# Four more weight tiles, six units ahead or in use, and units given back one by one, in a two-layer decoder trunk on one core

## The chip, the cores and the metric

The kernel runs on one core of one Trainium2 chip. The metric is the time of one execution on the device, in microseconds. The engines are called TensorE (PE, and PEld for its weight loads), VectorE (DVE), ScalarE (ACT), GpSimd (POOL) and SyncE (SP), as in the profile.

## The reference

Two layers work on 512 tokens of width 1024. In each layer, `x` is normalised and multiplied by one wide input matrix, whose columns feed three mixers and their gates; the mixers' outputs are gated, projected, added up, multiplied by `w_out` and added to `x`:

```
h    = rmsnorm(x, norm_g)
proj = h @ w_in        # columns: rq rk rv rz | sq sk sv sz | cu cz | ga gb gc
y_a  = retention(rq, rk, rv)       * silu(rz)
y_b  = stick_breaking(sq, sk, sv)  * silu(sz)
y_c  = s5_ssm(cu)                  * silu(cz)   # with its own product, w_glu
merged = sigmoid(ga)*(y_a @ proj_a) + sigmoid(gb)*(y_b @ proj_b) + sigmoid(gc)*(y_c @ proj_c)
x    = x + merged @ w_out
```

Retention works in chunks of 128 tokens with 4 heads. Stick-breaking attention has 8 heads, four pairs here; it needs, for each query, a running product over the keys of sigmoid(-z), and multiplies it by sigmoid(z). The state-space mixer keeps 64 complex states for each of 32 groups of channels. All is float32.

## The kernel before, in words

**Weights.** All weights of both layers come as 196 units of 128 x 1024 numbers (98 a layer), in the order in which they are used. A unit is loaded by SP's queue into a tile `raw`. ScalarE rounds it into `wh` (line 318), VectorE subtracts that from `raw` and leaves the rest in `wl` (helper line 197): this pair is a unit that is made. Each product is then three matmuls, high by high, high by low, low by high (`three`). `raw`, `wh` and `wl` share one pool of W_TILES = 12 tiles of 4 KB per partition; a tile is free again when its last reader in the program has run. Up to RAW_BUFS = 4 tiles are `raw`, and up to W_BUFS = 4 units may be made and not yet given back: 4 x 2 + 4 = 12.

The class `Weights` counts: `made`, `free` (units given back), `loaded`. `room(n)` asks whether n more tiles fit, `fill()` makes units as long as `made < free + W_BUFS` and there is room, and loads after each, `take()` hands out the next unit and makes it if it isn't there.

**Pieces.** The program is written out by hand as a list of pieces, each of 24 matmuls of 512 columns (12 for the products with 4 blocks), and the order of instructions on every engine is the order in which they are written; the engines wait for each other by semaphores alone. ORDER_TEXT sets the order. A product *by tokens* (sk, sq, sv, cu, rq, rk, rv0, rv1, out0, out1) has four pieces, one for each 128 tokens, and each piece reads all four of its units: `token_major` takes four units ahead of its first piece and gives them back, all four, at the end of its fourth. A product *by channels* (sz, gb, cz, gc, ga, rz, pa, and glu, pb, pc with two pieces to a unit) takes one unit, which is given back after the piece (`channel_piece`, counted at the end of the main loop's turn).

Numbered from 0, a layer has the pieces sk 0 to 3, sq 4 to 7, sv 8 to 11, sz:1 12, ..., gb:6 23, cu 24 to 27, cz:0 28, ..., rq 48 to 51, rk 52 to 55, rv0 56 to 59, rv1 60 to 63, glu from 64, ..., out0 100 to 103, out1 104 to 107; the second layer's sk begins with 108.

**What is written around a piece.** In the main loop's turn for a piece, first come the steps that are due in it: the generators of the mixers and evacuations, each of which says after how many pieces it goes on. A step that says 0 has issued small matmuls and goes on "late", in the same turn behind the piece: it evacuates what they gave. Then comes the piece itself, `m()`, then the late steps, then `W.fill()`, then "background" work (the state-space coefficients), until the estimated load of VectorE or GpSimd for this turn is reached.

So, for one piece, ScalarE and VectorE see: due steps, late steps, conversions of weights, background.

**The steps that the text speaks of.**
- Stick-breaking, `sb_pair`: for each head, scores `z` (TensorE), `kp` and `w` = sigmoid of both signs (ScalarE, lines 1047 and 1048), a scan along `kp` and a product into `w` (VectorE, line 1051 and the helper), in a late step; later the transposes `wt` of these `w` (TensorE, line 1068, `turn`) as a due step ahead of a piece. Pair 3 has its second head's scores in piece 27 and the transposes of it ahead of piece 28.
- State-space: `U` (line 867) evacuates cu; `win` (line 729) is a matrix turned by TensorE; `ut` (line 883) is `U` turned, and `S<-ut,win` uses both a piece later; `mt` (line 801) are copies on GpSimd of `kk`, which VectorE makes.
- Normalising, `normalise`: a token block of `x` is turned by TensorE (line 398), and ScalarE and VectorE evacuate it as `hh` (line 421) and `hl`, the operands of all products of the layer. At the start this is written out with the first four conversions between (`first_x`); in the last pieces of out1 it makes the next layer's.

Of the kernel before, what the change touches and what calls it, by code (L numbers as in the profile page):

```python
# [21 lines left out]
NT = 4  # L22
# [12 lines left out]

K = dict(

    nw=12, w=4, raw=4, b=48,

    sb0=0, sb_gap=4, ssm0=6, ssm_gap=3, ret0=9, ret_gap=3, x0=-3, x1=2, ret_pre=4, lead=9,  # L40

# [145 lines left out]
def trunk(ctx: ExitStack, tc, x_in, w_in, par_in, bc_in, ng_in, cst_in, rope_in, out):  # L187
    nc = tc.nc
# [33 lines left out]
    def pmm():  # L222
        return ps_mm.tile([P, 512], F32, tag="mm", name="mm")
# [47 lines left out]
    def then(gen):  # L271

        spawn(gen, now[0] + 1, True)
# [61 lines left out]
    W = Weights()  # L335
    between = []

    def three(ps, a, b, first, last):

        MM(ps, a[0], b[0], start=first, stop=False)  # L340
        MM(ps, a[0], b[1], start=False, stop=False)
        MM(ps, a[1], b[0], start=False, stop=last)
# [10 lines left out]
    def token_major(lhs, evac):  # L353

        units = []

        def piece(t):
            if not units:
                units.extend(W.take() for _ in range(4))
            ps = pmm()  # L360
            for k in range(8):
                if k == 4 and between:
                    between.pop()()
                w = units[k // 2]
                sl = slice(512 * (k % 2), 512 * (k % 2) + 512)
                three(ps, lhs(k, t), (w[0][:, sl], w[1][:, sl]), k == 0, k == 7)
            if t == NT - 1:
                W.free += 4
            then(evac(t, ps))

        return [lambda t=t: piece(t) for t in range(NT)]
# [1020 lines left out]
```

## Time and profile before

| | |
|---|---|
| three runs | 1311.26 us median (1310.98 to 1312.12) |
| the profiled execution | 1311.17 us, span 1309.5 us |
| TensorE busy | 1271.7 us (97%), granted clock 0.992 over the span |
| VectorE, ScalarE, GpSimd busy | 855.6 us (65%), 537.6 us (41%), 382.5 us (29%) |
| DMA queues | two of kind hardware_dynamic (29,664 and 7,632 packets), two of kind instruction (50 and 29) |

A row of a timeline gives the start in microseconds from the span's start, the duration, engine, line, operation, the tile written and those read, their shapes, a count of instructions merged, and in brackets the idle time of the engine just before and what ended it. For a matmul the streamed operand stands first: `mm<-wh,hh` is a product by tokens, `mm<-hh,wh` one by channels. A row of a stretch gives its length and then busy time and number of instructions of PE, PEld, DVE, ACT and POOL, the granted clock of TensorE as a share of 2.4 GHz, the busy share of the DMA engines and GB/s.

### The profile page before, as it was taken

How to read it: one execution, taken by the hardware profiler on the slowest of the kernel's cores; microseconds unless marked ns; L12 is line 12 of the kernel's file. 1: busy time of each engine (PE TensorE's matmuls, PEld its weight loads, DVE VectorE, ACT ScalarE, POOL GpSimd, SP SyncE). 2: the span in 40 equal slices, each digit the busy share in tenths (PEclk: the TensorE clock that was granted, in tenths of full speed). 3: DMA queues.
4: the chain of work that ended last, by engine and by line, in shares of the span. 5: the costliest groups of instructions: out<-in, count | busy, mean ns of one | idle time of the engine just before them, and what ended most of it. 6: DMA issues, size and time to landing. Idle time of an engine off the chain costs nothing. (4 is left out here: it accounts for less than half of the span.)

```text
span 1309.5 us, 16640 instructions
## 1 busy us (share of the span) xinstructions
PE 1271.7 (97%) x6360; PEld 1048.5 (80%) x6360; DVE 855.6 (65%) x1189; ACT 537.6 (41%) x919; POOL 382.5 (29%) x452
## 2 busy tenths in 40 slices
PE   6989989999999999999999999899999999999998
PEld 5867768788887888888888877788888878888887
DVE  5997678776785438556365576789657844575542
ACT  5445534445343534332244445344534534423311
POOL 3340036638442012000042000584555311210000
PEclk9989989999999999999999999899999999999999
DMA  6232221222322322234433222122241232222342
GB/s 223 90 124 77 65 65 49 81 81 89 119 68 65 104 77 77 81 97 141 161 118 127 81 65 71 43 81 65 84 127 65 65 120 90 65 74 88 97 135 75
DMA packets 37375, 120.05 MB, mean 92 GB/s; under 512 B 4144, under 2 KB 4528, under 8 KB 37296
## 3 DMA queue, kind: packets, MB, share of 16 engines
q1 hardware_dynamic: 29664, 105.40, 25.2%
q10 hardware_dynamic: 7632, 13.59, 3.1%
q8 instruction: 50, 0.82, 0.3%
q14 instruction: 29, 0.24, 0.1%
HBM read 114.78 MB, written 4.19 MB: 91 GB/s over the span
## 5 line engine op out<-in xcount | busy, mean ns | idle before, releaser
L197 DVE TENSOR_TENSOR wl<-raw,wh 128x1024 fp32r<-128x1024 f32 x196 | 251.6, 1294 | 114.6 <-ACT wh L318 111.8
L197 PE MATMUL mm<-hh,wh 128*128 128x512 f32 x640 | 256.0, 400 | 0.0
L197 PE MATMUL mm<-hh,wl 128*128 128x512 f32 x640 | 251.2, 393 | 4.9 <-DVE wl L197 4.9
L197 PE MATMUL mm<-hl,wh 128*128 128x512 f32 x640 | 250.7, 392 | 0.0
L318 ACT ACTIVATE wh<-raw 128x1024 fp32r<-128x1024 f32 x196 | 205.8, 1057 | 86.7 <-PE mm L197 38.9
L197 PE MATMUL mm<-wh,hh 128*128 128x512 f32 x512 | 207.5, 405 | 0.9 <-ACT hh L421 0.9
L197 PE MATMUL mm<-wl,hh 128*128 128x512 f32 x512 | 202.6, 396 | 4.3 <-DVE wl L197 4.3
L197 PE MATMUL mm<-wh,hl 128*128 128x512 f32 x512 | 202.0, 395 | 0.0
L197 PEld LDWEIGHTS mm<-hh,wl 128*128 128x128 f32 x640 | 120.8, 189 | 32.2 <-DVE wl L197 6.3
L197 PEld LDWEIGHTS mm<-hh,wh 128*128 128x128 f32 x640 | 121.0, 189 | 25.1 <-issue 1.6
L197 PEld LDWEIGHTS mm<-hl,wh 128*128 128x128 f32 x640 | 121.0, 189 | 23.5
L197 PEld LDWEIGHTS mm<-wl,hh 128*128 128x128 f32 x512 | 104.5, 204 | 24.5 <-DVE wl L197 7.8
L197 PEld LDWEIGHTS mm<-wh,hh 128*128 128x128 f32 x512 | 104.5, 204 | 19.0 <-ACT hh L421 1.3
L197 PEld LDWEIGHTS mm<-wh,hl 128*128 128x128 f32 x512 | 104.2, 204 | 18.4 <-DVE hl L197 0.3
L1051 DVE TENSOR_TENSOR_SCAN kp<-kp,zero 128x511 f32<-128x511 f32 (+1 forms) x64 | 67.6, 1076 | 26.2 <-ACT kp L1047 26.1
L994 ACT ACTIVATE gate<-mm 128x512 f32<-128x512 f32 x48 | 28.6, 596 | 114.2 <-PE mm L197 114.2
L197 POOL TENSOR_SCALAR ms<-ss 128x8 f32<-128x8 f32 (+3 forms) x56 | 19.1, 341 | 181.5 <-DVE ss L824 100.6
L197 POOL TENSOR_TENSOR rs<-ms,mhalf 128x8 f32<-128x8 f32 (+3 forms) x56 | 64.6, 1154 | 4.7
L1033 POOL CAST qd<-qd 64x512 fp32r<-64x512 f32 x16 | 16.3, 1016 | 134.1 <-ACT qd L1028 133.7
L822 ACT ACTIVATE sq<-mm 128x512 f32<-128x512 f32 x32 | 19.0, 593 | 84.6 <-PE mm L197 84.5
L197 PE MATMUL mm<-wl,mgh 128*128 128x512 f32 x128 | 50.1, 391 | 0.2
L197 PE MATMUL mm<-wh,mgh 128*128 128x512 f32 x128 | 49.9, 390 | 0.0
(253 smaller groups left out, 2263.2 us busy)
## 6 DMA issues: line engine op xcount, KB each, us to landing
raw<-in_w SPq DMA_DIRECT2D x196, 512.0 KB, 3.5
x<-in_x SPq DMA_DIRECT2D x8, 256.0 KB, 7.3
rope<-in_rope ACTq DMA_DIRECT2D x8, 256.0 KB, 3.7
xh<-in_x ACTq DMA_DIRECT2D x8, 256.0 KB, 4.4
x<-xh ACTq DMA_DIRECT2D x8, 256.0 KB, 2.0
xh<-x ACTq DMA_DIRECT2D x8, 256.0 KB, 4.6
out<-xh ACTq DMA_DIRECT2D x8, 256.0 KB, 2.1
gB<-in_ng SPq DMA_DIRECT2D x2, 256.0 KB, 5.8
```

What stands on the lines that cost most here:

```text
L197: return f(*a, **k)
L318: ACT(wh, raw, AF.Copy)
L822: ACT(s2, ps, AF.Square)
L994: ACT(sg, ps, AF.Sigmoid)
L1033: nc.gpsimd.tensor_copy(out=qd[h][o, :], in_=qd[h][r, :])
L1051: nc.vector.tensor_tensor_scan(v, v, zero1.to_broadcast([P, n - 1]), 1.0, ALU.mult, ALU.add)
```

## The change

The pool has 16 tiles instead of 12, and up to six units may be made and not given back. The room comes from a part of SBUF that is set aside for descriptors written by GpSimd, which the kernel doesn't use: 512 bytes per partition of it are left. And a product by tokens gives a unit back, and calls `fill()`, in its fourth piece after every second of the eight blocks, instead of giving back all four behind it.

```
--- before.py
+++ after.py
@@ -35,7 +35,7 @@
 
 K = dict(
 
-    nw=12, w=4, raw=4, b=48,
+    nw=16, w=6, raw=4, b=48,
 
     sb0=0, sb_gap=4, ssm0=6, ssm_gap=3, ret0=9, ret_gap=3, x0=-3, x1=2, ret_pre=4, lead=9,
 
@@ -364,8 +364,10 @@
                 w = units[k // 2]
                 sl = slice(512 * (k % 2), 512 * (k % 2) + 512)
                 three(ps, lhs(k, t), (w[0][:, sl], w[1][:, sl]), k == 0, k == 7)
-            if t == NT - 1:
-                W.free += 4
+                if t == NT - 1 and k % 2:
+
+                    W.free += 1
+                    W.fill()
             then(evac(t, ps))
 
         return [lambda t=t: piece(t) for t in range(NT)]
@@ -1378,7 +1380,7 @@
     from concourse.bass_utils import run_bass_kernel_spmd as _run
 
     ins = _layout({k: np.asarray(v) for k, v in inputs.items()})
-    nc = _bacc.Bacc("TRN2", target_bir_lowering=False, num_devices=1)
+    nc = _bacc.Bacc("TRN2", target_bir_lowering=False, num_devices=1, dynamic_dma_scratch_size=512)
     arrays, args = {}, []
     for name in _INS:
         a = np.ascontiguousarray(ins[name])
```

## Rows read from the trace of the kernel before

**Rows 1.** TensorE's waits: engine, line, waited for; us in total, times, longest.

```profile
PE wt L1068 <- DVE w L197: 13.5, 8, 3.1
...
PE mm L197 <- DVE wl L197: 9.2, 7, 3.3
```

**Rows 2.** Stretches of time; busy time by engine, granted clock, DMA share, GB/s.

```profile
80.00:100.00 20.00, 15.91 (x60) 12.16 (x59) 17.98 (x18) 9.77 (x13) 12.93 (x13) 0.83 0.35 117
...
90.89:104.72 13.83, 12.26 (x47) 9.90 (x48) 11.03 (x13) 8.15 (x12) 2.46 (x3) 0.76 0.13 39
...
189.00:198.00 9.00, 9.00 (x39) 8.19 (x37) 4.22 (x5) 1.49 (x6) 0.72 (x1) 0.77 0.19 60
...
220.00:240.00 20.00, 19.06 (x93) 14.70 (x93) 15.78 (x17) 9.47 (x20) 16.86 (x19) 1.00 0.40 132
...
400.00:420.00 20.00, 17.88 (x83) 14.23 (x82) 12.71 (x10) 9.24 (x14) 7.29 (x4) 1.00 0.33 106
```

**Rows 3.** TensorE's timeline, sv to sz and pair 0: start, duration, tile<-operands, [idle].

```profile
92.46 0.79 PE L197 MATMUL mm<-hh,wl 128*128 128x512 f32 x1 [3.30 <-DVE wl L197]
...
107.12 1.04 PE L1068 MATMUL wt<-ident,w 128*128 128x128 f32 x8
```

**Rows 4.** The page's groups, the subtraction: busy, mean ns | idle before, releaser.

```profile
L197 DVE TENSOR_TENSOR wl<-raw,wh 128x1024 fp32r<-128x1024 f32 x196 | 251.6, 1294 | 114.6 <-ACT wh L318 111.8
```

**Rows 5.** VectorE's timeline in the first stage.

```profile
30.84 0.69 DVE L824 TENSOR_REDUCE ss<-sq 128x8 f32<-128x512 f32 x1 [0.81 <-ACT sq L822]
...
90.89 5.53 DVE L197 TENSOR_TENSOR wl<-raw,wh 128x1024 fp32r<-128x1024 f32 x4
...
104.29 0.43 DVE L197 TENSOR_TENSOR w<-w,kp 128x255 f32<-128x255 f32 x1
```

**Rows 6.** ScalarE's timeline in piece 27, the last of cu.

```profile
214.89 1.12 ACT L729 ACTIVATE win<-T 128x512 f32<-128x512 f32 x2
...
218.28 1.06 ACT L318 ACTIVATE wh<-raw 128x1024 fp32r<-128x1024 f32 x1 [0.73 <-PE mm L197]
...
227.70 0.76 ACT L867 ACTIVATE U<-mm 128x128 f32<-128x128 f32 x4
```

**Rows 7.** TensorE's timeline: after two stick-breaking waits, pieces 27 and 28, and S.

```profile
188.40 2.18 PE L1068 MATMUL wt<-ident,w 128*128 128x128 f32 x9 [2.41 <-DVE w L197]
...
197.06 0.40 PE L197 MATMUL mm<-wh,hl 128*128 128x512 f32 x1
...
222.31 0.40 PE L197 MATMUL mm<-wh,hl 128*128 128x512 f32 x1
...
222.55 1.62 PE L1068 MATMUL wt<-ident,w 128*128 128x128 f32 x10
...
230.32 0.39 PE L197 MATMUL mm<-hh,wl 128*128 128x512 f32 x1
...
356.44 2.00 PE L197 MATMUL S<-ut,win 128*128 128x64 f32 x16
```

**Rows 8.** VectorE's timeline: first scan and last product of two heads.

```profile
118.50 1.27 DVE L1051 TENSOR_TENSOR_SCAN kp<-kp,zero 128x127 f32<-128x127 f32 x2
...
121.27 0.42 DVE L197 TENSOR_TENSOR w<-w,kp 128x255 f32<-128x255 f32 x1
...
216.54 2.73 DVE L1051 TENSOR_TENSOR_SCAN kp<-kp,zero 128x127 f32<-128x127 f32 x2 [1.08 <-ACT kp L1047]
...
222.48 0.42 DVE L197 TENSOR_TENSOR w<-w,kp 128x255 f32<-128x255 f32 x1
```

**Rows 9.** GpSimd's timeline behind piece 27.

```profile
224.30 6.47 POOL L801 COPY mt<-kk 32x256 f32<-32x256 f32 x8 [2.47 <-DVE kk L197]
```

**Rows 10.** Late steps of pieces 51 and 107, and what stands ahead of piece 108.

```profile
349.22 1.55 ACT L883 ACTIVATE ut<-T 64x256 f32<-64x256 f32 x4
...
659.94 1.06 ACT L421 ACTIVATE hh<-T 128x512 fp32r<-128x512 f32 x2
...
664.38 1.03 PE L398 MATMUL T<-ident,xn 128*128 128x128 f32 x8
```

More of the change, by code (lines that the diff above doesn't have):

```diff
@@ L36 @@
 K = dict(
-    nw=12, w=4, raw=4, b=48,
+    nw=16, w=6, raw=4, b=48,
     sb0=0, sb_gap=4, ssm0=6, ssm_gap=3, ret0=9, ret_gap=3, x0=-3, x1=2, ret_pre=4, lead=9,
@@ L366, in piece @@
                 three(ps, lhs(k, t), (w[0][:, sl], w[1][:, sl]), k == 0, k == 7)
-            if t == NT - 1:
-                W.free += 4
+                if t == NT - 1 and k % 2:
+                    W.free += 1
+                    W.fill()
             then(evac(t, ps))
@@ L1380 @@
     ins = _layout({k: np.asarray(v) for k, v in inputs.items()})
-    nc = _bacc.Bacc("TRN2", target_bir_lowering=False, num_devices=1)
+    nc = _bacc.Bacc("TRN2", target_bir_lowering=False, num_devices=1, dynamic_dma_scratch_size=512)
     arrays, args = {}, []
```

## The prediction

> **What bounds the kernel now.** I read the shares of busy time first: TensorE is busy nearly throughout, so the time is its stream of products plus the places where it stands. Then TensorE's list of waits [rows 1]: two causes carry most of it, `wt` (transposes of stick-breaking weights) waiting for VectorE's `w`, and products waiting for the low part `wl` of a weight unit. Only the second is a matter of weights being late. The list has no places, so next came stretches of time [rows 2]: 80 to 100 has 15.91 us of products and a clock of 0.83; 220 to 240 loses 0.94 us, 400 to 420 loses 2.12, and the second layer repeats these two once each. TensorE's timeline names the pieces: sv to sz:1 at 92.46 [rows 3], cu to cz:0 near 225, rv0 to rv1 near 410. Each is an end of a product by tokens, which holds all four units that may exist until its last piece. Last came what ScalarE and VectorE do in those last pieces, because the change puts instructions there.
>
> **The change part by part.** *Six units instead of four.* The conversions per piece are worked out from the program's counters: a piece that makes one unit still makes one, the last piece of each product by tokens still makes four, but piece 0 makes two more, and from there each unit is made two units earlier. So the first two units of the next product are ready before its turn.
>
> (a) sv to sz:1. The 3.30 us wait at 92.46 goes [rows 3]; what is late next is VectorE itself. The two subtractions added in piece 0 cost it 2 x 1.29 = 2.6 us [rows 4], and it has hardly a gap from 30.84 on; the idle 0.81 us before 30.84 takes some of that up, so at piece 11 it is about 1.8 us late: the four subtractions that begin at 90.89 begin at 92.7 [rows 5]. From there to the last `w` that pair 0 needs (104.29 + 0.43) VectorE works 11.03 of 13.83 us [rows 2]; the rest was waiting for results of TensorE, which now comes earlier. So that `w` is there at 92.7 + 11.0 = 103.7, and the `wt` of 107.12 [rows 3] can run 3.4 us sooner. Gain 3.4 us. Bounds: nothing (VectorE as far behind as TensorE), and 5.7 us (the 3.30 us and some 2.4 us of products at the low clock behind it: 0.76 over the 13.83 us).
>
> (b) rv0 to rv1: the 2.12 us of 400 to 420 [rows 2] go, in both layers, since units one and two are ready and three and four are wanted only half a piece later. Gain 4.2 us; bounds 2 and 4.2.
>
> (c) Piece 0 itself. The two added conversions stand on ScalarE and VectorE ahead of the normalising of token blocks 2 and 3. I take nothing, as block 2 is wanted only by piece 2; bounds 0 and the 1.8 us by which VectorE then runs late.
>
> *Giving back one by one.* Before, the four conversions of a last piece came after that piece's "late" steps (evacuations of small products that are issued ahead of the piece). Now they are issued inside the piece, so ahead of the late steps, on ScalarE and VectorE alike. And with 6 x 2 + 4 = 16 tiles all taken, a conversion can only write into the two tiles of the unit just given back: it waits until TensorE has read that unit. The fourth therefore starts when the piece ends, and everything late is queued behind it. That ScalarE's queue holds later work back shows in rows 6: `U` could be evacuated after the last product of the piece at 222.31 [rows 7], and ran at 227.70, behind the conversions. What stands there in each last piece:
>
> (d) cu, piece 27 (and its twin in layer 2): the late steps are two copies `win`, the sigmoids `kp` and `w` of pair 3's second head, and VectorE's scans and products on them, and TensorE's next instructions are the transposes `wt` of just these. Today `win` starts at 214.89 [rows 6], the scans and products run from 216.54 to 222.90 [rows 8], and `wt` follows at 222.55 without a wait [rows 7]: no cover is left. After: the last read of the fourth unit is the product at 222.31; its conversion runs from 222.5 to 223.56 (1.06 long, as the one at 218.28 [rows 6]); the scan starts as far behind `win` as now, 216.54 - 214.89 = 1.65, so at 225.2. The chain of scans and products takes 118.50 to 121.69 = 3.19 us in pair 0 and 6.36 us here [rows 8]. GpSimd, busy beside it today, is idle for 2.47 us before 224.30, and what it does then waits for steps behind this chain [rows 9]; so I take 3.19: `w` at 228.4. One transpose runs a little before; nine are left. The nearest row for nine transposes and 24 products after such a wait is 188.40 to 197.06 + 0.24 = 8.9 us [rows 7], in which the granted clock was 0.77 [rows 2], that is, part of it at 1.2 GHz. So piece 28 ends at 228.4 + 8.9 = 237.3, against 230.32 + 0.23 = 230.55, with today's 0.94 us for `wl` already in the latter. Loss 6.7 us, twice: 13.4. Bounds per place: 4.4 (no time at the low clock: less 0.9 for the transposes and 1.4 for the products) and 9.9 (chain of 6.36).
>
> The two lengths of the chain are 3.2 us apart, and a rule says which to take. The Trainium skill, "SBUF — State Buffer", section "Who interferes with whom": a VectorE instruction with two SBUF inputs shuts out, and is shut out by, a GpSimd instruction that reads SBUF. By the row at the same place the time would be 1326.6, by the rule, with GpSimd idle, it stays as summed below.
>
> (e) rq, piece 51, twice: the late step is the copies `ut`, 1.55 us [rows 10], wanted by `S` at 356.44 [rows 7]. The piece's last read is at 354.4, the conversion ends at 355.5, `ut` at 357.1. Loss 0.7 us each, 1.4; bounds 0 and 1.5.
>
> (f) out1, piece 107, once: the late step is `hh` and then `hl` of the next layer's first token block [rows 10]. After the piece's end come 0.2 + 1.06 us for the conversion, 1.29 for its subtraction on VectorE and 0.6 for the first `hl`, 3.2 us; TensorE wants it some 1.4 us after the end (eight transposes of block 1, 1.03 [rows 10], and two products). Loss 1.8 us; bounds 0 and 2.3.
>
> sk, sv, rv1 and out0 have no late steps in the last piece. sq, rk and rv0 have copies that nobody wants within a piece: nothing, hidden by pieces of 5.5 us; 0.5 each if the PSUM banks they hold ran out. The first piece of a product no longer makes a unit ahead of its late steps; nothing on the path waits for those there.
>
> *The scratch.* The page lists no queue whose descriptors GpSimd writes: nothing. The loads in SP's queue keep their order; at the start four more find fresh tiles, so no load waits longer than now.
>
> **Sum.** -3.4 - 4.2 + 13.4 + 1.4 + 1.8 = +9.0 us. The profiled execution took 1311.17 us (span 1309.5, 1.7 around it), 0.1 under the median of the runs, so 1320.2, say 1320.
>
> **The rivals.**
> 1. *Not slower: the late steps of piece 27 aren't held.* If its conversions wrote to tiles that are free early, they would run behind the piece's first `U`, from 215.0, and be done at 219.2; `w` would come at 219.2 + 1.65 + 3.19 = 224.0, 1.5 us after `wt` wants it, less the 0.94 saved: +0.6 at each place, and nothing for (e) and (f). -3.4 - 4.2 + 1.2: 1304.8. It decides by the end of the fourth conversion: before some 222.4 the gains win. For it: the wait of `wh` for TensorE is short today. Against: the count of sixteen. Chance 0.11.
> 2. *The clock doesn't fall behind the new waits, and the first stage gives back its whole 5.7 us.* 2 x 4.4 + 1.4 + 1.8 - 5.7 - 4.2 = +2.1: 1313.3. For it: VectorE is idle for 2.8 of the 13.83 us. Against: the stand in (d) is longer than the 3.30 us at 92.46, behind which the clock is down. Chance 0.15.
> 3. *GpSimd's work moves along with the chain*, which is 6.36 long again: 2 x 3.2 more, 1326.6. Against: rows 9. Chance 0.13.
> 4. *VectorE is the bound of the first stage,* and its 2.6 us push TensorE as far as the ready units pull: (a) is nothing, 1323.6. For it: 17.98 of 20 us in 80 to 100. Chance 0.13.
>
> My forecast has 0.48.
>
> **How the numbers follow.** The forecast, 3 and 4 are slower by over 0.2% (2.6 us, about what a measurement of this kernel tells from no change): 0.74. Of 2, two thirds lie within 0.2% and a third above. Slower 0.79, same 0.10, faster 0.11. The low end of the range is (d) at 4.4 with (a) at 5.7 and (e), (f) at nothing, 1310; the high end is rival 3, 1327. Rival 1 and a bit of both sides are left out.
>
> **What would show it.** Right: in the profile of the changed kernel no product waits for `wl` at sz:1, cz:0 and rv1; `wt` at the start of cz:0 waits over 5 us for `w` in both layers, with a clock below 1 behind it; ScalarE's order there is four `wh`, then `win`, then `kp`; `S` in rk waits about 0.7 us for `ut`, and the first products of layer 2 wait for `hl`. Wrong: the fourth `wh` of piece 27 done before its end, or `kp` ahead of it; then rival 1 holds. If the `wt` near 104 waits as long as sz:1 gained, rival 4 does.

## The result, and the profile after

The changed kernel takes 1325.01 us, median of four runs (1323.77 to 1325.37); beside it the kernel before took 1311.41 us (1310.98 to 1312.12). The ratio is 1.0101, with a 95% interval of 1.0084 to 1.0119: slower by 13.6 us. The forecast was 1320, its range 1310 to 1327. The profiled execution took 1325.37 us (span 1323.7), 14.2 more than that of before (1311.17).

TensorE's list of waits, as in [rows 1] (engine, line, what was waited for; us in total, times, longest). Line numbers from 369 on are two higher than before.

```profile
PE wt L1070 <- DVE w L197: 24.5, 12, 5.2
...
PE z L197 <- DVE ks L197: 4.3, 1, 4.3
PE T L400 <- DVE m L197: 3.3, 2, 1.7
PE mm L197 <- ACT hh L423: 1.6, 2, 0.8
PE S L197 <- ACT ut L885: 0.7, 2, 0.4
PE mm L197 <- DVE hl L197: 0.6, 1, 0.6
```

No product waits for `wl` any more (9.2 us in seven waits before). In its place `wt` waits 11.0 us longer, and the rows under it are new or longer. The stretches, as in [rows 2] (length, busy time by engine, granted clock):

```profile
80.00:100.00 20.00, 15.74 (x58) 12.17 (x57) 18.56 (x25) 9.35 (x13) 10.95 (x13) 0.83 0.37 115
...
220.00:240.00 20.00, 14.58 (x58) 11.80 (x59) 10.62 (x15) 8.85 (x18) 8.48 (x14) 0.83 0.32 106
...
420.00:440.00 20.00, 18.34 (x85) 14.92 (x84) 5.73 (x7) 7.61 (x12) 0.00 (x0) 1.00 0.13 32
...
860.00:880.00 20.00, 14.22 (x82) 13.10 (x81) 14.21 (x17) 10.57 (x23) 11.54 (x10) 0.92 0.34 106
```

80 to 100 is no better than before; 220 to 240 has 14.58 us of products where it had 19.06, and a clock of 0.83 where it had 1.00; its twin in layer 2, 860 to 880, has 14.22 where it had 19.02, and 0.92 where it had 1.00. The idle time behind rv0 has moved to 420 to 440 and is smaller (1.66 us for 2.12). TensorE's timeline names the places; the last number is the idle time ahead, and who ended it:

```profile
92.75 0.76 PE L197 MATMUL z<-ks,qd 128*128 128x512 f32 x1 [4.26 <-DVE ks L197]
...
108.84 1.26 PE L1070 MATMUL wt<-ident,w 128*128 128x128 f32 x10
...
228.96 0.45 PE L1070 MATMUL wt<-ident,w 128*128 128x128 f32 x1 [4.83 <-DVE w L197]
...
230.00 2.18 PE L1070 MATMUL wt<-ident,w 128*128 128x128 f32 x9 [0.59 <-DVE w L197]
...
365.27 1.77 PE L197 MATMUL S<-ut,win 128*128 128x64 f32 x14 [0.36 <-ACT ut L885]
...
423.67 0.63 PE L400 MATMUL T<-ident,m 128*128 128x128 f32 x4 [1.66 <-DVE m L197]
...
673.27 0.50 PE L197 MATMUL mm<-wh,hh 128*128 128x512 f32 x1 [0.76 <-ACT hh L423]
...
674.64 0.50 PE L197 MATMUL mm<-wh,hl 128*128 128x512 f32 x1 [0.64 <-DVE hl L197]
...
878.43 0.45 PE L1070 MATMUL wt<-ident,w 128*128 128x128 f32 x1 [5.19 <-DVE w L197]
```

What stands behind the wait at 228.96 is in ScalarE's timeline, to be held against [rows 6]:

```profile
219.70 1.06 ACT L318 ACTIVATE wh<-raw 128x1024 fp32r<-128x1024 f32 x1 [3.25 <-PE mm L197]
...
224.17 1.06 ACT L318 ACTIVATE wh<-raw 128x1024 fp32r<-128x1024 f32 x1 [0.34 <-PE mm L197]
225.13 1.07 ACT L731 ACTIVATE win<-T 128x512 f32<-128x512 f32 x2
226.09 0.60 ACT L1049 ACTIVATE kp<-z 128x512 f32<-128x512 f32 x1
```

Each `wh` starts when TensorE has read the unit before it; `win`, which stood ahead of them at 214.89, now comes behind the fourth. VectorE's timeline answers to [rows 5] in its first part and to [rows 8] in its second:

```profile
33.05 0.69 DVE L826 TENSOR_REDUCE ss<-sq 128x8 f32<-128x512 f32 x1 [0.81 <-ACT sq L824]
...
81.58 1.15 DVE L197 TENSOR_TENSOR dbl<-ci 128x128 f32<-128x128 f32 x1
...
91.92 0.69 DVE L197 TENSOR_TENSOR ks<-sqk,ks 64x512 fp32r<-64x512 f32 x1
...
94.07 4.89 DVE L197 TENSOR_TENSOR wl<-raw,wh 128x1024 fp32r<-128x1024 f32 x4
...
106.01 0.43 DVE L197 TENSOR_TENSOR w<-w,kp 128x255 f32<-128x255 f32 x1
...
220.79 1.41 DVE L197 TENSOR_TENSOR wl<-raw,wh 128x1024 fp32r<-128x1024 f32 x1 [3.94 <-ACT wh L318]
222.44 4.40 DVE L197 TENSOR_TENSOR wl<-raw,wh 128x1024 fp32r<-128x1024 f32 x3 [0.24 <-ACT wh L318]
226.76 1.26 DVE L1053 TENSOR_TENSOR_SCAN kp<-kp,zero 128x127 f32<-128x127 f32 x2
...
229.52 0.42 DVE L197 TENSOR_TENSOR w<-w,kp 128x255 f32<-128x255 f32 x1
...
415.93 7.00 DVE L197 TENSOR_TENSOR wl<-raw,wh 128x1024 fp32r<-128x1024 f32 x4
422.84 1.29 DVE L197 TENSOR_TENSOR m<-m,m 128x512 f32<-128x512 f32 x2
```

GpSimd's answers to [rows 9]:

```profile
231.34 2.78 POOL L803 COPY mt<-kk 32x256 f32<-32x256 f32 x8 [8.21 <-DVE kk L197]
```

**Where the 14.2 us are.** Every piece begins with the same product in every kernel here, so the start of each piece, subtracted between two traces, gives a sum place by place (us against the profiled execution of before; "together", "one by one" and "two a turn" are experiments below; "sk to cu" ends where the second piece of cu, piece 25, begins):

```
place                                     said    changed  together  one by one  two a turn
                                                            (e1)      (e2)        (e7)
first product                              -       -0.3     -1.0      -0.8        +0.3
sk to cu              (a) and (c)         -3.4     +1.7     +0.2      +1.4        -4.4
cu to pb              (d), layer 1        +6.7     +6.6     -0.3      +6.8        -0.7
rk                    (e), layer 1        +0.7     +0.6      0.0      +0.6         0.0
rv0, rv1              (b), layer 1        -2.1     -1.0     -1.0       0.0        -2.9
out0                                       0       -0.4     -0.4       0.0        -0.4
start of layer 2      (f)                 +1.8     +1.9      0.0      +2.0         0.0
sk to cu, layer 2                          0       -0.5     +0.5      +0.4        +0.4
cu to pb              (d), layer 2        +6.7     +6.5     -0.3      +7.0        -0.8
rk                    (e), layer 2        +0.7     +0.6      0.0      +0.6         0.0
rv0, rv1              (b), layer 2        -2.1     -1.1     -1.1       0.0        -2.9
out0                                       0       -0.4     -0.4       0.0        -0.4
all                                       +9.0    +14.2     -3.9     +18.0       -11.8
```

At rk, rv0, rv1, out0 and the start of layer 2 kernels with the same code agree within 0.1 us. The stretch from sk to cu is different: three kernels below (e5, e6, e8) issue the same instructions up to piece 14, and end it at -1.3, 0.0 and -1.7; two others, e3 and e9, do so too, and end it at -2.1 and +0.5. One profile of that stretch is good to some 2.5 us, no better.

### The profile page after: what moved, and what is told of

It reads as the page before. It is cut to its first block, busy times and chain, and to the rows that moved or that the text cites. A ratio compares the mean times of both kernels' runs of the same rounds, so it can differ in the third digit from the quotient of the medians.

```text
span 1323.7 us, 16599 instructions
## 1 busy us (share of the span) xinstructions
PE 1275.1 (96%) x6360; PEld 1053.3 (80%) x6360; DVE 849.3 (64%) x1189; ACT 538.2 (41%) x919; POOL 374.5 (28%) x452
## 5 line engine op out<-in xcount | busy, mean ns | idle before, releaser
L1053 DVE TENSOR_TENSOR_SCAN kp<-kp,zero 128x511 f32<-128x511 f32 (+1 forms) x64 | 63.0, 1005 | 23.4 <-ACT kp L1049 23.2
L1070 PE MATMUL wt<-ident,w 128*128 128x128 f32 x160 | 26.5, 313 | 24.5 <-DVE w L197 24.5
```

What stands on the lines that cost most here:

```text
L1053: nc.vector.tensor_tensor_scan(v, v, zero1.to_broadcast([P, n - 1]), 1.0, ALU.mult, ALU.add)
L1070: nc.tensor.transpose(pt[:, i * P : i * P + P], wblk(h, b, kb), ident)
```

## The experiments

**Order or amount: four kernels.** The change does two things, so each was run alone. First the tiles and units without the new order (e1; diffs are against the changed kernel unless said otherwise):

```diff
-                if t == NT - 1 and k % 2:
-                    W.free += 1
-                    W.fill()
+            if t == NT - 1:
+                W.free += 4
```

> Sixteen tiles and six units as in the changed kernel, but the four units of a product by tokens are given back together after its last piece, so that the conversions stand behind the late steps again. Theory (order: conversions issued inside the last piece hold up the late steps): the waits of wt for w at cz:0, of S for ut and of the products for hh and hl go, and with them 6.6 + 6.6 + 0.6 + 0.6 + 1.9 us; the waits for wl at cz:0 (0.94 us, twice) stay away too, and the first stage stays 1.4 us late: 1311.3 + 1.4 - 1.9 - 2.1 = 1308.7. Rival (the six units themselves cost it: more conversions early, tiles taken from elsewhere, loads that come at other times): 1320 or more.

Measured: 1308.59 us, ratio to before 0.9978 (0.9968 to 0.9988). TensorE's waits in it:

```profile
PE wt L1068 <- DVE w L197: 13.6, 9, 3.1
...
PE z L197 <- DVE ks L197: 4.3, 1, 4.3
PE T L398 <- DVE m L197: 3.4, 2, 1.7
```

The waits of (d), (e) and (f) are gone, and those of `z` and `T` are as in the changed kernel. The sixteen tiles and six units together gain 2.9 us; the loss is the order.

Then the order without the tiles and units (e2):

```diff
-    nw=16, w=6, raw=4, b=48,
+    nw=12, w=4, raw=4, b=48,
...
-    nc = _bacc.Bacc("TRN2", target_bir_lowering=False, num_devices=1, dynamic_dma_scratch_size=512)
+    nc = _bacc.Bacc("TRN2", target_bir_lowering=False, num_devices=1)
```

> The kernel before (twelve tiles, four units, scratch as it was) with only the giving back one by one. Theory (order): twelve tiles are just as full (4 x 2 + 4), so the loss at cz:0, at rk and at layer 2 stays whole: +13.2 + 1.2 + 1.9; rv1 gains the 1.0 us per layer that it gains in the changed kernel; the first stage has no added subtractions, so sz:1 starts sooner and the transposes wt behind it wait as much longer, sum 0: 1311.3 + 16.3 - 2.1 = 1325.5. Rival (the six units cost it): 1307 to 1311, since nothing but the order of the conversions is changed.

Measured: 1328.55 us, ratio 1.0129 (1.0112 to 1.0145), +17.0. The losses (d), (e) and (f) are all there, place by place as in the changed kernel. Two parts of what was expected were wrong: rv1 gains nothing (the last units still come too late with four), so (b) belongs to the six units alone; and the first stage is 1.4 us late without any added subtraction. The two halves add up: -2.9 + 17.0 = 14.1, against 13.6 measured together.

Third, is it the hold (a conversion waits for the unit just given back) or only the place in the queue? With four units in sixteen tiles, two units' worth of tiles are free when the first conversion is issued (e3):

```diff
-    nw=16, w=6, raw=4, b=48,
+    nw=16, w=4, raw=4, b=48,
```

> The changed kernel with four units ahead or in use instead of six: 4 x 2 + 4 = 12 of the 16 tiles, so that a conversion inside the last piece finds two units' worth of free tiles and needn't wait for the read of the unit just given back. Theory (the hold by full tiles makes the loss, not the order alone): the fourth conversion of piece 27 is done at mid-piece, the late steps run at most 1.5 us late, so cz:0 loses 0.6 us or less per layer, ut and hh nothing; with rv1 -1.0 per layer: 1309 to 1311. Rival (the order alone is enough: four conversions ahead of the late steps on two engines, wherever they write): 4.2 us of conversions per place, 1320 or more.

Measured: 1319.92 us, ratio 1.0068 (1.0054 to 1.0083). Neither theory: +8.4. ScalarE's timeline of piece 27, then VectorE's, then TensorE's:

```profile
212.45 2.02 ACT L318 ACTIVATE wh<-raw 128x1024 fp32r<-128x1024 f32 x2
216.07 1.06 ACT L318 ACTIVATE wh<-raw 128x1024 fp32r<-128x1024 f32 x1 [1.60 <-PE mm L197]
217.48 1.07 ACT L318 ACTIVATE wh<-raw 128x1024 fp32r<-128x1024 f32 x1 [0.35 <-PE mm L197]
...
219.41 0.60 ACT L1049 ACTIVATE kp<-z 128x512 f32<-128x512 f32 x1
```

```profile
213.56 3.24 DVE L197 TENSOR_TENSOR wl<-raw,wh 128x1024 fp32r<-128x1024 f32 x2 [0.57 <-ACT wh L318]
217.16 3.88 DVE L197 TENSOR_TENSOR wl<-raw,wh 128x1024 fp32r<-128x1024 f32 x2 [0.36 <-ACT wh L318]
220.97 2.12 DVE L1053 TENSOR_TENSOR_SCAN kp<-kp,zero 128x127 f32<-128x127 f32 x2
```

```profile
224.03 0.30 PE L1070 MATMUL wt<-ident,w 128*128 128x128 f32 x1 [3.77 <-DVE w L197]
```

The hold is shorter, not gone: two conversions run at once, the third and the fourth still wait 1.60 and 0.35 us for TensorE. ScalarE is done with them at 218.55, before TensorE begins to wait (224.03 - 3.77 = 220.26), and `kp` is written by 220.01. VectorE has four subtractions of 1.6 to 1.9 us ahead of the scans, with GpSimd's products beside them until 222; the scans begin at 220.97 and take 2.12 us instead of 1.26. So both queues carry the loss: ScalarE's brings `kp` some 6 us later against the start of the piece than in the kernel before, VectorE's and GpSimd's add some 0.9 us before the scans and as much in them. cu to pb loses 5.9 us in layer 1 and 4.3 in layer 2, against 6.6 and 6.5 in the changed kernel; (e) is 0.0, (f) 0.8. The two layers wait alike here (4.50 and 4.51 us in all); what differs is the granted clock behind the wait, 0.73 from 224.03 to 236.83 and 0.85 from 872.46 to 883.73. So the place in the two queues, with two of the four conversions still held, makes most of (d); (e) comes with the full hold alone. What no hold at all would leave of (d) was not run.

Fourth, the changed kernel with the in-piece conversions left out in cu alone (e4):

```diff
                     W.free += 1
-                    W.fill()
+                    if inside:
+                        W.fill()
...
-            cu=token_major(hstride, cu_evac),
+            cu=token_major(hstride, cu_evac, False),
```

> The changed kernel, but in the two pieces of cu's end the conversions are issued after the late steps (the units are counted as given back one by one all the same). Theory (the loss at cz:0 is these conversions alone): 1325.0 - 12.2 (the steps of the changed kernel at cu and cz, 6.3 + 5.9) - 1.9 (the waits for wl of the kernel before, which stay away) = 1310.9, with S waiting for ut and products for hh as before. Rival (the loss at cz:0 comes from the work running 1.4 us late since the first stage, or from GpSimd beside the chain): 1318 or more.

Measured: 1311.48 us, ratio 1.0001 (0.9992 to 1.0010). cu to pb is -0.3 and -0.2, every other place as in the changed kernel ((e) 0.6, (f) 2.0). The two ends of cu are 13 us of the loss; (e) and (f) stay.

**The first stage: five kernels.** (a) came out wrong, so the question was what the 3.30 us wait of [rows 3] had been. The scratch alone was run as a control (e11, against the kernel before):

```diff
-    nc = _bacc.Bacc("TRN2", target_bir_lowering=False, num_devices=1)
+    nc = _bacc.Bacc("TRN2", target_bir_lowering=False, num_devices=1, dynamic_dma_scratch_size=512)
```

> The kernel before with only the smaller DMA scratch. Prediction's step: nothing, the same time as before within 0.2%: 1308 to 1314. Rival (a transfer needs that scratch): slower.

Measured: 1310.62 us, ratio 1.0000 (0.9990 to 1.0009). The scratch costs nothing. Its TensorE timeline says more, for its instructions are those of the kernel before. First the row of `z` in the kernel before, then two of e11:

```profile
87.86 0.47 PE L197 MATMUL z<-ks,qd 128*128 128x512 f32 x1 [0.79 <-DVE ks L197]
```

```profile
89.61 0.77 PE L197 MATMUL z<-ks,qd 128*128 128x512 f32 x1 [3.65 <-DVE ks L197]
...
92.21 0.80 PE L197 MATMUL mm<-hh,wl 128*128 128x512 f32 x1 [0.32 <-DVE wl L197]
```

In the profile of before, `z` waited 0.79 us for `ks` and the product behind it 3.30 for `wl`: together 4.09. Here it is 3.65 + 0.32 = 3.97, and 4.26 + 0 in the changed kernel. One lateness of VectorE, met under two names.

The tiles alone (e5), and six units only from piece 14 on (e6), both against e1:

```diff
-    nw=16, w=6, raw=4, b=48,
+    nw=16, w=4, raw=4, b=48,
```

```diff
+            ahead = 4 if now[0] < 14 else W_BUFS
-            while self.made < min(self.free + W_BUFS, L * NU) and self.room(2):
+            while self.made < min(self.free + ahead, L * NU) and self.room(2):
```

> The four more tiles alone: sixteen tiles, four units ahead or in use, given back together, conversions behind the late steps. Theory (in the first stage VectorE is the bound, and six units cost it two subtractions; the tiles by themselves only free ScalarE, which in the kernel before waits behind VectorE for a tile at 92.44): the first stage gains 1.6 us, as where four units were tried with sixteen tiles, and nothing else changes: 1309.5. Rival (what is late in the changed kernel's first stage is the contention between GpSimd and VectorE at 78 to 90, whichever the number of units): no gain, 1311.5 or more.

> As with the units given back together (1308.6), but only four units ahead until piece 14, and six from there. Theory (the two added subtractions in piece 0 are what makes the first stage late, since VectorE is its bound): the first stage gains 1.6 us against the kernel before instead of losing 1.2 (beyond the start), the rest stays at -3.0: 1306.8. Rival (the phase in which GpSimd and VectorE meet decides): the first stage as late as with six, 1308.6.

Measured: 1309.70 us, ratio 0.9992 (0.9983 to 1.0001), and 1306.76 us, ratio 0.9971 (0.9959 to 0.9983). The tiles alone are within the uncertainty of no change. The second has the expected median, but against 0.9978 with six from the start the difference is not resolved, and its own profile has the first stage at 0.0, not at the -1.6 that was to bring it. The same edit in the changed kernel itself (e9):

> The changed kernel with only four units ahead until piece 14 (so without the two added conversions of piece 0), six from there; giving back one by one throughout. Theory (VectorE is the bound of the first stage, and the two added subtractions are what it is late by): the first stage ends 1.5 to 2 us sooner than in the kernel before instead of 1.7 us later, as with four units in sixteen tiles: 1325.0 - 3.3 = 1321.7. Rival (the added subtractions are absorbed, and it is the meeting of GpSimd and VectorE between 78 and 90 that makes the first stage late): 1324 or more.

Measured: 1322.84 us, ratio 1.0091 (1.0076 to 1.0106), 12.5 us over before on that chip, where the changed kernel was 13.6 over. The added subtractions cost 1.1 us, a third of what was expected, and the two intervals overlap: not shown. Its profile has sk to cu at +0.5, where -1.5 to -2 was expected.

What GpSimd beside VectorE has to do with it: its background products held back until piece 14, in the changed kernel (e10) and in e1 (e12).

```diff
+        def wait14():
+            while now[0] < 14:
+                yield "end"
+
-        background = chain(tables(), coef.gen) if l == 0 else coef.gen
+        background = chain(tables(), wait14(), coef.gen) if l == 0 else coef.gen
```

> The changed kernel, with GpSimd's background products for the state space coefficients held back until piece 14 in layer 1 (in the changed kernel they run beside VectorE's last table steps, 80 to 90). Theory (VectorE's instructions there last up to four times as long beside GpSimd, and that is why ks comes at 91.92 and z waits 4.3 us): ks comes some 4 us sooner, the wait of z goes, and the first stage ends 3 to 5 us sooner: 1320 to 1322. Rival (the two added subtractions are the whole delay; contention only changes which instruction pays): z's wait shrinks, and wt for w waits as much longer, 1324 or more.

> Sixteen tiles, six units, given back together (1308.6), with GpSimd's background products held back until piece 14 in layer 1. In the kernel with two conversions a turn the first stage ended 4 us sooner, and there these products had moved behind piece 12 too. Theory (that gain is the moved GpSimd work): 1304.5. Rival (it is the two subtractions fewer ahead of pair 0's scans): 1308 or more.

Measured: 1323.88 us, ratio 1.0101 (1.0084 to 1.0118), the same ratio as the changed kernel; and 1306.97 us, 0.9974 (0.9963 to 0.9985), against 0.9978 without the holding back. In the first, `z` no longer waits, and piece 13 begins 5.3 us sooner than in the kernel before (counted from the first product); but piece 18 only 0.4 sooner, for GpSimd's products now meet the scans of a later pair. VectorE's timeline of the first of the two, then TensorE's:

```profile
81.17 0.28 DVE L197 TENSOR_TENSOR dbl<-ci 128x128 f32<-128x128 f32 x1
```

```profile
117.77 0.30 PE L1070 MATMUL wt<-ident,w 128*128 128x128 f32 x1 [2.44 <-DVE w L197]
119.38 2.17 PE L1070 MATMUL wt<-ident,w 128*128 128x128 f32 x9 [1.31 <-DVE w L197]
```

No gain in either, as the rivals had it (1324 and 1308 were their bounds; the kernel before ran 1.1 us lower here than beside e1). The contention moves the wait from one instruction to another.

**A better version: two kernels.** At rv1 four subtractions in a row (7.00 us at 415.93) stand ahead of the `m` that TensorE waits for. With six units, two are enough at once. E1 with at most two conversions a turn (e7):

```diff
+            end = self.made + 2
-            while self.made < min(self.free + W_BUFS, L * NU) and self.room(2):
+            while self.made < end and self.made < min(self.free + W_BUFS, L * NU) and self.room(2):
```

> As with the units given back together (1308.6), but at most two conversions in one turn, so that the four after a product by tokens are spread over two turns. Theory (at rv1 the T of m waits 1.7 us because four subtractions, 7 us, stand ahead of m on VectorE): both waits of T for m go or shrink below 0.5, -2.4 to -3.3, and in the first stage only two subtractions stand ahead of the scans of pair 0, -1 or so: 1304.5 to 1306. Rival (the last two units come too late instead): products wait for wl at the second half of the next product, 1308.6 or more.

Measured: 1298.30 us, ratio 0.9906 (0.9892 to 0.9920), 6 to 8 us better than expected. VectorE's timeline at rv1, and two stretches:

```profile
402.49 4.54 DVE L197 TENSOR_TENSOR wl<-raw,wh 128x1024 fp32r<-128x1024 f32 x2
406.95 0.68 DVE L197 TENSOR_TENSOR m<-m,m 128x512 f32<-128x512 f32 x1
407.55 2.53 DVE L197 TENSOR_TENSOR wl<-raw,wh 128x1024 fp32r<-128x1024 f32 x2
```

```profile
80.00:100.00 20.00, 20.00 (x94) 16.29 (x94) 18.63 (x36) 12.83 (x19) 3.79 (x5) 1.00 0.48 155
...
400.00:420.00 20.00, 20.00 (x95) 16.50 (x94) 10.59 (x8) 7.04 (x10) 5.94 (x4) 1.00 0.32 105
```

`m` comes between two pairs of subtractions, `T` does not wait, and 400 to 420 is full: -2.9 a layer where the changed kernel had -1.0. The first stage gains 4.4 us, and the last table steps and GpSimd's products have moved behind piece 12 there. Which of the edit's effects on that stage brings it is not settled; GpSimd's products alone do not (e12). Both edits together, four units and no limit until piece 14, then six and two a turn (e8):

```diff
+            ahead = 4 if now[0] < 14 else W_BUFS
+            end = self.made + (4 if now[0] < 14 else 2)
-            while self.made < min(self.free + W_BUFS, L * NU) and self.room(2):
+            while self.made < end and self.made < min(self.free + ahead, L * NU) and self.room(2):
```

> Both together: four units ahead and conversions as they come until piece 14, then six and at most two a turn. Theory (the gains are at different places and add up): 1306.8 - 2.4 to 3.3 = 1304. Rival (six units and two a turn pay in the same waits): no better than the better of the two alone.

Measured: 1301.58 us, ratio 0.9934 (0.9921 to 0.9946). From rv0 on it is as e7; in the first stage it has -1.7 where e7 has -4.4. So the two don't add up, and e7 stays the best kernel here.

## Why the prediction was right, and where not

Direction and kind were right, the size 5 us short: 1325.0 against 1320. The sum by its own steps:

- **(d)**, the largest term, +13.4: measured 6.6 + 6.5 = 13.1. In layer 1 the mechanism is there row by row: four `wh`, the fourth at 224.17 behind TensorE's read, then `win`, then `kp`. The chain of scans and products, taken as 3.19 us, is 226.76 to 229.94 = 3.18, with GpSimd idle beside it for 8.21 us, until `kk` was there; rival 3's 6.36 did not come. Layer 2 repeats it: the fourth `wh` at 873.28, the chain from 876.23 to 879.41. `wt` waits 4.83 + 0.59 us in layer 1 and 5.19 + 0.59 in layer 2, over 5 us as said. By the Trainium skill, "SBUF — State Buffer", section "Who interferes with whom", VectorE is not shut out while GpSimd reads nothing; the trace agrees, 3.18. What the prediction had not seen is that most of the loss does not need the full hold: rival 1 priced early conversions at +0.6 a place. With two of the four conversions held and done before the piece's end (e3), the places lost 5.9 and 4.3. In its layer 1 the conversions waited 1.95 us for TensorE, the scans stood some 0.9 us behind VectorE's subtractions, which rival 1 had not counted, and the chain took 4.04 us (220.97 to 225.01) beside GpSimd instead of 3.19.
- **(e)** +1.4: measured 1.2, of which the wait of `S` for `ut` is 0.36 a layer, half of the 0.7 that was named as a sign. **(f)** +1.8: 1.9, the wait split between `hh` (0.76) and `hl` (0.64).
- **(c)** nothing: small new waits of `T` and products for `qn` (0.9 us in all), and sv's second piece 1.7 us later against the first product, in the changed kernel; no such steps with four units. It was inside the bounds, and disappears in the lateness of the whole stage.
- **(a)** -3.4: measured, with (c), +1.7. This step failed. It took 3.30 us for a wait for weights, with VectorE's lateness as a second thing behind it. But `z` stands ahead of sz:1 and reads `ks` from VectorE, so TensorE could not come sooner, and nothing behind it either. The four subtractions began at 94.07, not 92.7: VectorE was 2.2 us late by 33.05 already (30.84 before). The idle 0.81 us, which was to take up part of the two subtractions, is still there: ScalarE's `sq`, which ends it, ran at 32.43 instead of 30.23. Then GpSimd's products stretched the table steps ahead of `ks`. The last `w` was ready at 106.4, not 103.7. Rival 4 (VectorE is the bound, (a) is nothing) is what the runs bear out, though not by the sign it named: `wt` at 108.84 does not wait, `z` does. It gave 1323.6. How much of the +1.7 the two added subtractions cost stays open: 1.1 by e9, within its uncertainty.
- **(b)** -4.2: measured -2.1. The wait for `wl` went, as said, but the step did not ask what the four conversions, still a block, then stand ahead of: `T` waits 1.66 us for `m`. Spread over two turns the whole gain and 0.8 more a layer is there (e7), so the mechanism was right and its end was cut off by a wait behind it.
- Not in the sum: -0.4 in each out0, and -0.5 from sk to cu in layer 2.

(a) at +1.7 for -3.4 is 5.1 us, (b) 2.1 more, together 7.2; the -1.3 not in the sum, -0.3 at the first product and some -0.4 in (d), (e) and (f) leave 5.2, which is the difference between +9.0 and +14.2.

## What to carry to other kernels

A refill that is issued as soon as its buffer is given back stands in the engines' queues ahead of all that is issued later, so list what is late behind it on every engine it uses before asking whether its buffer is free. A wait named after a weight may be one engine's lateness: look whether the instruction just ahead waits for the same engine, and add the two. When a pool grows, use the room to break up the burst that follows a release: that was worth more here than giving back early.

## What the runs showed of the hardware

How much GpSimd and VectorE cost each other at one place changes from execution to execution. The same table step, `dbl<-ci` of 128x128, took 0.28 us with GpSimd idle (e10, 81.17) and 1.15 beside GpSimd's products of 1.06 to 1.11 us (changed kernel, 81.58): VectorE's instruction lasted about as long as one of GpSimd's. In the profile of before, GpSimd paid part: its `bi,co_re` product took 1.39 us there, but 1.07 in e11, which runs the same instructions, and 1.06 in the changed kernel. Against the changed kernel, VectorE finished `ks` 4.9 us sooner in the kernel before, only 2.2 of which it had been ahead at 33. VectorE's row of `ks` and GpSimd's product in the kernel before, then the product in e11:

```profile
86.73 0.99 DVE L197 TENSOR_TENSOR ks<-sqk,ks 64x512 fp32r<-64x512 f32 x1
...
87.25 1.39 POOL L197 TENSOR_TENSOR ct<-bi,co_re 128x512 f32<-128x512 f32 x1
```

```profile
84.80 1.07 POOL L197 TENSOR_TENSOR ct<-bi,co_re 128x512 f32<-128x512 f32 x1
```

The Trainium skill, "SBUF — State Buffer", section "Who interferes with whom", says that the order of issue, not the operation, decides which of the two stands; these rows agree in that the same operation pays in one execution and not in the other, but they do not show the order of issue. So a difference of one or two us in such a stretch says little in a single profile, while the differences at rk, rv and out0 repeat to 0.1 us.
